# Hybrid S5 / differential attention / HGRN2 layer on one core: rows of x split and turned by DMA transposes, the norm's weight multiplied into the projection's weights, mixed channels loaded once per chunk

## The chip, the core and the metric

One core of a Trainium2 chip runs the whole program in one launch. The metric is the device time of an execution in microseconds, here the median of several runs. TensorE (PE) does the matmuls, VectorE (DVE), ScalarE (ACT) and GpSimd (POOL) the rest; SyncE (SP) issues most DMAs. Each engine works its instructions off in the order in which the program lists them for it.

## What is computed

One layer on x of 2048 rows and 1024 channels, in float32. The reference, cut to what matters:

```python
def rmsnorm(x, g):
    r = lax.rsqrt(jnp.mean(x * x, axis=-1, keepdims=True) + EPS)
    return x * r * g
...
h = rmsnorm(x, norm_mix_g[l])
proj = h @ w_in[l]
u, dq, dk, dv, cq, cf, ci, cg = split_projection(proj)   # 256, 3 x 384, 4 x 384 columns
y_a = s5_mixer(u, ...)
y_b = diff_attention(dq, dk, dv, ...)
y_c = hgrn2_mixer(cq, cf, ci, cg, ...)
mix = jnp.concatenate([y_a, y_b, y_c], axis=-1)
x = x + mix @ w_out[l]
h = rmsnorm(x, norm_ffn_g[l])
x = x + conv_glu_ffn(h, w_up, w_gate, conv_w, conv_b, w_down)
return rmsnorm(x, final_norm_g)
```

The change concerns h, the three places that multiply h by columns of w_in, and the product with w_out.

## The kernel before

**Products.** A float32 factor is held as two fp16 parts, a high part and the rest. `split` (L52) makes them: ACT writes the high part (L55), then DVE the low part in one operation (L63, or L61 where the scale is 1), or, with `pool=True`, POOL in two: a scaling in place (L58) and a subtraction (L59). `three` (L91, matmuls at L96) adds high x high, low x high and high x low. Weights are scaled by 1024 (`WS`) before the split, and results by its inverse.

**Order.** The program is written as generators that take turns, and a scheduler that works with a simulated timeline then fixes the order on every engine. Buffers come from pools with a fixed number each; who wants a buffer waits for its last reader.

**Stage A** (`phase_a`, L160) takes x in 16 row tiles of 128x1024, in four chunks j of 512 rows. `norm(j)` (L204) squares four tiles (ACT L216, two of the first chunk DVE L211), takes 1/sqrt (POOL's power at L72 and three small DVE operations), and scales the rows in place (ACT L227, DVE L229, POOL L233). Then PE turns each 128x128 block (L251, 8 blocks of 4 tiles a chunk) into PSUM tiles `a_pt`, which are split with the norm's weight g as scale (L255) into `a_h`: channels on partitions, tokens along the row. The chunk goes to DRAM as `Hd` (L259). For each of its tiles 24 matmuls (`a_pm`) give the 256 columns of u, which go to `Ud` (L269). `load_w` (L177) loads blocks of 128 columns of w_in into `a_wst` (two buffers) and splits them, two for u (`a_wu`) and nine for q, k and v (`a_w`). Between the tiles stand steps of the S5 branch: its parameters on DVE, and rotations of C on POOL (L537).

**QKV.** `proj` (L288) reads `Hd` chunk by chunk into `a_h2` (L291) and multiplies by `a_w` (`a_p`, to `QKd` and `Vd`). Beside it run the S5 branch, with its tables on POOL (L567 to L584) and its scans (tiles `s_w`, `s_ya`), and the splits of the first FFN weights.

**Attention and HGRN** are woven together. HGRN works in three passes `pr` over two heads each; at the start of a pass (`proj(u)`, j == 0) it loads four blocks of w_in (L1121) into `g_wst`, of which there is one buffer, and splits them into `g_w`, of which there is one, ACT first and DVE behind it (L1125). `load_h` (L1101) reads 256 tokens of `Hd` for each half chunk. The products are `g_pq` and `g_pv`. Attention turns its weights by DMA: `t_sc`, high and low part side by side, through `dma_start_transpose` into `t_wt` (L898).

**Second output projection.** The first FFN half runs, and within it `second` (L1960) makes the product with w_out for chunks 2 and 3. `project` (L1467) goes over two halves n of the output columns, and for each over four groups q of 256 channels: the mixed channels `o_y` are read from `Yd` (L1478, two DMAs), a block of w_out into `o_wst` (L1480) and split into `o_w` (L1488), then 24 matmuls follow (L1493). The rest is the second half of the FFN.

## Time and profile before

| | us |
|---|---|
| median of 3 runs | 2719.52 |
| lowest, highest run | 2718.45, 2723.11 |
| the profiled execution's own time | 2723.9 |
| its span (first to last instruction in the trace) | 2722.1 |
| mean granted TensorE clock | 0.934 |
| busy: PE, DVE | 2408.0, 1873.5 |
| busy: POOL, ACT | 1350.7, 1316.9 |

A line of the profile names the source line, the engine, the operation, the tile written and the tiles read ("a_h<-a_pt,a_g"), and the count; a group has the minimum, median and maximum of one instruction in ns. "[7.02 <-ACT g_w L55]" behind an instruction is idle time of its engine before it in us, and what ended it. A line "PE o_pm L1493: 16.9, 6" among waits gives us and how often. SPq is SP's queue of DMA issues. The table of stretches gives, for each, busy time of PE, its weight loads, DVE, ACT and POOL, the granted clock, the share of the 16 DMA engines, and GB/s.

### The profile page before, as it was taken

The numbers are of one execution on the slowest core, as the hardware profiler recorded it, in microseconds if no ns is written. First come the engines' busy times: TensorE is split into PE (matmuls) and PEld (weight loads), VectorE is DVE, ScalarE is ACT, GpSimd is POOL, SyncE is SP. The second block draws the span as 40 slices with busy tenths as digits, with TensorE's granted clock in tenths as the row PEclk, the third lists the DMA queues.
The fourth block names the chain that finished last, engine by engine and source line by source line (L and its number), as shares of the span: only waits on it lengthen the run. The fifth ranks groups of instructions, "written<-read, shape, count | busy, mean of one in ns | idle before, by whom it ended". The sixth has DMA issues, their size and how long they took to land.

```text
span 2722.1 us, 42584 instructions
## 1 busy us (share of the span) xinstructions
PE 2408.0 (88%) x15438; PEld 1354.2 (50%) x15438; DVE 1873.5 (69%) x3401; ACT 1316.9 (48%) x2470; POOL 1350.7 (50%) x1149
## 2 busy tenths in 40 slices
PE   5998898888888889769988898598979999999998
PEld 4655556766766764334443444243434444444444
DVE  7467756688869885597788998865455655545565
ACT  6333344667757663564466766633235433333321
POOL 5688612455444542367677677515313344444280
PEclk8899898888989989879999999699989999999999
DMA  7676555467456666655466665688784655554733
GB/s 240 230 214 207 167 161 126 94 133 143 104 125 137 132 135 177 161 122 182 150 182 169 183 173 170 207 276 256 266 312 148 204 168 154 155 148 136 286 99 123
DMA packets 556740, 473.07 MB, mean 174 GB/s; under 512 B 277297, under 2 KB 433265, under 8 KB 555505
## 3 DMA queue, kind: packets, MB, share of 16 engines
q1 hardware_dynamic: 534352, 429.97, 56.0%
q10 hardware_dynamic: 22176, 40.38, 4.0%
q8 instruction: 121, 1.98, 0.3%
q14 instruction: 91, 0.74, 0.1%
HBM read 290.35 MB, written 125.83 MB: 153 GB/s over the span
## 4 chain that ended last, share of the span: by engine, by line
PE 22%; DVE 15%; issue 8%; POOL 7%; ACT 7%; DMA 6%; SPq 1%; ACTq 0%; DVEq 0%; POOLq 0%
PE f_pd L1786 10%; PE f_pm L96 7%; POOL f_k L1863 2%; DVE f_a L61 2%; DMA f_dst<-in_w_down_dram 2%; DVE t_sc L836 2%; DVE f_t L1617 2%; PE o_pm L1493 2%; PE o_pe L1411 2%; DVE t_sc L867 1%; DVE f_w L63 1%; POOL f_u L1863 1%; ACT f_t L1615 1%; ACT f_t L1910 1%; ACT t_sc L848 1%
## 5 line engine op out<-in xcount | busy, mean ns | idle before, releaser
L96 PE MATMUL f_pm<-f_q,f_w 128*128 128x512 f16 x3696 | 836.8, 386 | 30.0 <-DVE f_u L1863 9.2
L96 PEld LDWEIGHTS <-f_w 128*128 128x128 f16 x3696 | 363.3, 99 | 487.5 <-issue 70.1
L1786 PE MATMUL f_pd<-f_dw,f_da 128*128 128x512 f16 x1848 | 407.1, 382 | 2.7 <-DVE f_r L1764 1.5
L891 POOL TENSOR_TENSOR t_sc<-t_sc 128x1024 f16<-128x1024 f32 (+7 forms) x144 | 250.6, 1753 | 302.3 <-ACT t_sc L890 279.1
L1786 PEld LDWEIGHTS <-f_da 128*128 128x128 f16 x1848 | 181.1, 98 | 226.2 <-issue 14.5
L832 PE MATMUL t_ps<-t_k,t_q 96*128 96x512 f16 (+2 forms) x480 | 165.9, 372 | 94.6 <-DVE t_mx L836 80.2
L848 ACT ACTIVATE t_sc<-t_sc,t_nm 128x128 f32<-128x128 f32 (+7 forms) x192 | 230.5, 1201 | 6.6 <-DVE f_a L61 1.1
L836 DVE CUSTOM_DVE_ANT_0 t_sc<-t_ps,t_base,t_mx 128x512 f32<-128x512 f32 (+3 forms) x288 | 185.2, 643 | 18.9 <-PE t_ps L832 10.8
L61 DVE TENSOR_TENSOR f_a<-f_t,f_a 128x512 f16<-128x512 f32 x132 | 154.8, 1192 | 48.3 <-ACT f_a L55 47.8
L913 PEld LDWEIGHTS <-t_wt 128*128 128x128 f16 x2448 | 106.3, 101 | 121.3 <-DMA t_wt<-t_sc 50.4
L867 DVE SCALAR_TENSOR_TENSOR t_sc<-t_sc,t_a 128x1024 f32<-128x1024 f32 (+7 forms) x144 | 164.6, 1169 | 1.6
L96 PE MATMUL g_pq<-g_h,g_w 128*128 128x256 f16 x1152 | 159.2, 299 | 5.1 <-DVE g_sg L1160 2.7
L1863 POOL TENSOR_TENSOR f_t<-f_t,f_t 128x512 f32<-128x512 f32 x66 | 101.6, 1553 | 123.1 <-ACT f_a L55 108.8
L913 PE MATMUL t_po<-t_v,t_wt 128*128 128x64 f16 x2448 | 120.5, 198 | 47.2 <-DMA t_wt<-t_sc 42.4
L96 PE MATMUL g_pv<-g_w,g_h 128*128 128x256 f16 x1152 | 150.3, 288 | 9.2 <-ACT g_w L55 9.2
L1863 POOL TENSOR_TENSOR f_k<-f_k,f_k 128x512 f32<-128x512 f32 x88 | 124.5, 1414 | 51.5 <-ACT f_halo L1907 25.4
L1617 DVE SCALAR_TENSOR_TENSOR f_t<-f_u,f_cw,f_t 128x1024 f32<-128x1024 f32 x88 | 124.1, 1410 | 33.1 <-ACT f_t L1615 32.3
L836 DVE CUSTOM_DVE_ANT_0 t_sc<-t_ps,t_base 128x512 f32<-128x512 f32 (+2 forms) x192 | 120.4, 631 | 34.4 <-PE t_ps L832 13.7
L890 ACT CAST t_sc<-t_sc 128x1024 f16<-128x1024 f32 (+7 forms) x144 | 111.4, 792 | 64.4 <-DVE t_sc L867 63.4
L55 ACT ACTIVATE f_w<-f_sum 128x512 f16<-128x512 f32 x110 | 69.2, 629 | 146.4 <-DVE f_sum L139 62.2
L96 PEld LDWEIGHTS <-g_w 128*128 128x128 f16 x1152 | 121.3, 107 | 36.2 <-issue 6.4
L96 PEld LDWEIGHTS <-g_h 128*128 128x128 f16 x1152 | 116.8, 103 | 36.8 <-issue 10.8
(335 smaller groups left out, 4475.4 us busy)
## 6 DMA issues: line engine op xcount, KB each, us to landing
f_w<-Wd SPq DMA_DIRECT2D x231, 256.0 KB, 3.0
Wd<-f_w SPq DMA_DIRECT2D x154, 256.0 KB, 2.1
Ad<-f_a ACTq DMA_DIRECT2D x154, 256.0 KB, 2.7
f_da<-Ad SPq DMA_DIRECT2D x42, 768.0 KB, 4.9
g_h<-Hd SPq DMA_DIRECT2D x24, 1024.0 KB, 6.7
f_dst<-in_w_down_dram SPq DMA_DIRECT2D x48, 512.0 KB, 4.9
...
```

The source lines that it names most:

```text
L61: nc.vector.tensor_tensor(out=lo, in0=src, in1=hi, op=ALU.subtract)
L96: nc.tensor.matmul(out=out, lhsT=lhs(a, k), rhs=rhs(b, k), start=(n == 0), stop=(n == 3 * nk - 1))
L832: nc.tensor.matmul(out=ps[:, 0:k1 - k0], lhsT=qt[:, c, 128 * (i % 4):128 * (i % 4) + 128], rhs=H.k[:, c, k0:k1], start=True, stop=True,)
L836: V.tensor_tensor_reduce(out=sc[c][:, k0:k1], in0=ps[:, 0:k1 - k0], in1=bs[:, k0:k1], scale=1.0, scalar=-3e38 if j == 0 else mx[:, c, j - ...
L848: nc.scalar.activation(out=sc[c][:, 0:L], in_=sc[c][:, 0:L], func=AF.Exp, scale=SLOPES[h], bias=nm[:, c:c + 1], accum_out=H.la[:, c, n_:n_ ...
L867: V.scalar_tensor_tensor(out=sc[0][:, k0:k1], in0=sc[1][:, k0:k1], scalar=a[:, 1:2], in1=sc[0][:, k0:k1], op0=ALU.mult, op1=ALU.add,)
L890: nc.scalar.copy(hl[:, k0:k1], sc[0][:, k0:k1])
L891: nc.gpsimd.tensor_tensor(out=hl[:, LM + k0:LM + k1], in0=sc[0][:, k0:k1], in1=hl[:, k0:k1], op=ALU.subtract,)
L913: nc.tensor.matmul(out=po, lhsT=wt[:, w, b, :], rhs=vt[:, b, 64 * v:64 * v + 64], start=(b == 0 and w + v == 0), stop=(b == i and w == 1),)
L1617: V.scalar_tensor_tensor(out=t0, in0=u[:, c:n + c], scalar=cw[:, c, m:m + 1], in1=t0, op0=ALU.mult, op1=ALU.add,)
L1786: nc.tensor.matmul(out=ps[t], lhsT=a[:, q, x, tk], rhs=w[:, y, q, :], start=(first and q + x + y == 0), stop=(last and q == n - 1 and y == 1),
L1863: eng.tensor_tensor(out=o, in0=a, in1=b, op=op)
```

## The change

**Stage A.** `turn(i)` takes the place of the transposes on PE: for each row tile ACT writes the high part of x·r and DVE the low part into `a_hl` (128x2048 fp16, three buffers), and one DMA transpose on SP turns the tile into `a_h`, with no norm weight in it. Norms are taken one tile at a time for the first four, then in pairs, all squares on ACT. x has seven buffers in place of eight; PSUM has four `a_pm` and no `a_pt`. In place of g in h, every block of w_in is multiplied by `gw` = 1024·g before its split (`scaled`), on POOL, or on DVE for the first block. `Hd` is stored as four tiles of [part, 128-channel group, 128 tokens] for each chunk; the matmuls that read 256 or 512 tokens read them in pieces of 128, and HGRN's reads get one contiguous piece per partition.

**HGRN.** Its 12 blocks get the same multiplication on POOL, in place in `g_wst`, ahead of the split.

**Second output projection.** `o_y` is loaded for n == 0 only, in four buffers instead of two, and `o_w` has two instead of three.

```diff
+    def scaled(self, f, eng):
+        eng.tensor_tensor(
+            out=f, in0=f, in1=self.gw.rearrange("p (k o) -> p k o", o=1).to_broadcast([128, KD, 128]),
+            op=ALU.mult,
+        )
...
# load_w in phase_a
-            K.split(dst[:, 0], dst[:, 1], f[:, :, 0:n], WS, pool=c0 > 0)
+            K.scaled(f, nc.gpsimd if c0 > 0 else nc.vector)
+            K.split(dst[:, 0], dst[:, 1], f[:, :, 0:n], 1.0, pool=c0 > 0)
...
-            xp = pool("a_x", 8)
+            xp = pool("a_x", 7)
+            lp = pool("a_hl", 3)
-            pt = pool("a_pt", 3, space=PSUM)
-            pm = pool("a_pm", 2, space=PSUM)
+            pm = pool("a_pm", 4, space=PSUM)
...
+            def turn(i):
+                j, t = divmod(i, 4)
+                if t == 0:
+                    hs[j] = hp.tile([128, 4, 2, KD, 128], F16, tag="h", name="a_h")
+                xt, r = xs.pop(i), rs.pop(i)
+                hl = lp.tile([128, 2, D], F16, tag="hl", name="a_hl")
+                nc.scalar.activation(out=hl[:, 0], in_=xt, func=AF.Copy, scale=r)
+                nc.vector.scalar_tensor_tensor(
+                    out=hl[:, 1], in0=xt, scalar=r, in1=hl[:, 0], op0=ALU.mult, op1=ALU.subtract
+                )
+                nc.sync.dma_start_transpose(
+                    out=hs[j][:, t].rearrange("p a k c -> p (a k) c"),
+                    in_=hl.rearrange("p a d -> p (a d)"),
+                )
+                load_x(i + 7)
...
-                        nc.tensor.transpose(
-                            ps[:, t * 128:t * 128 + 128], xs[4 * j + t][:, k * 128:k * 128 + 128],
-                            K.ident,
-                        )
-                    K.split(h[:, 0, k, :], h[:, 1, k, :], ps, g[:, k:k + 1])
...
+            for i in range(S // 128):
+                j, t = divmod(i, 4)
+                if i < 3:
+                    norm(i + 1, 1)
+                elif i % 2 and i + 1 < S // 128:
+                    norm(i + 1, 2)
+                if i + 1 < S // 128:
+                    turn(i + 1)
+                h = hs[j]
+                ps = pm.tile([128, 256], F32, tag="pm", name="a_pm")
+                three(nc, ps, lambda a, k: h[:, t, a, k, :], lambda b, k: wu[:, b, k, :], KD)
+                ut = op.tile([128, 256], F32, tag="u", name="a_u")
+                nc.scalar.activation(out=ut, in_=ps, func=AF.Copy, scale=IWS)
+                nc.sync.dma_start(out=Ud[128 * i:128 * i + 128, :], in_=ut)
+                if t == 3:
+                    nc.sync.dma_start(out=Hd[j], in_=hs.pop(j))
...
# load_h and proj(u) in HGRN
-            nc.sync.dma_start(out=h, in_=Hd[j, :, :, :, 256 * a:256 * a + 256])
+            nc.sync.dma_start(out=h, in_=Hd[j, :, 2 * a:2 * a + 2])
-                    K.split(w[:, 0, :, cc], w[:, 1, :, cc], f, WS)
+                    K.scaled(f, nc.gpsimd)
+                    K.split(w[:, 0, :, cc], w[:, 1, :, cc], f)
...
# project and second
+                if n == 0:
+                    y = yp.tile([128, 2, 2, CH], F16, tag="y", name="o_y")
+                    for k in range(2):
+                        nc.sync.dma_start(
+                            out=y[:, k], in_=Yd[2 * q + k, :, :, j * CH:(j + 1) * CH])
+                    ys[q] = y
+                y = ys[q]
-            yp, wp, st = pool("o_y2", 2, "left"), pool("f_w2", 3, "left"), pool("f_st2", 2, "left")
+            yp, wp, st = pool("o_y2", 4, "left"), pool("f_w2", 2, "left"), pool("f_st2", 2, "left")
```

The scheduler puts the instructions in another order. Three places follow, before and after. First, SP's queue at the end of stage A (`a_h_1430`, `a_h_2235`, and after the change `a_h_1310`, `a_h_2115`, are the first two chunks read back for QKV). Before:

```order
32 L259 DMA Hd<-a_h 128x8192
33 L269 DMA Ud<-a_u 128x256 x4
34 L179 DMA a_wst<-in_w_in_dram 128x8x128 x2
35 L291 DMA a_h_1430<-Hd 128x8192
36 L291 DMA a_h_2235<-Hd 128x8192
37 L259 DMA Hd<-a_h 128x8192
```

and after:

```order
62 L188 DMA a_wst<-in_w_in_dram 128x8x128
63 L242 DMA_TRANSPOSE a_h<-a_hl 128x16x128 x2
64 L188 DMA a_wst<-in_w_in_dram 128x8x128
65 L272 DMA Ud<-a_u 128x256
66 L274 DMA Hd<-a_h 128x8192
67 L272 DMA Ud<-a_u 128x256
68 L188 DMA a_wst<-in_w_in_dram 128x8x128
69 L296 DMA a_h_1310<-Hd 128x8192
70 L272 DMA Ud<-a_u 128x256
71 L296 DMA a_h_2115<-Hd 128x8192
```

The first read of `Hd` has moved from ahead of the last chunk's write to behind it, and behind the last two transposes and the last block of w_in.

Second, POOL at the start of HGRN, where the first pass's weights come (`g_mk`, `t_base`: masks and positions). Before:

```order
360 L1036 MEMSET g_ones 128x512
361 L1046 AFFINE_SELECT g_mk<-g_ones 128x64 x2
362 L1050 AFFINE_SELECT g_mk<-g_mk 128x64 x2
363 L1046 AFFINE_SELECT g_mk<-g_ones 128x64
364 L1058 AFFINE_SELECT g_mk_3689<-g_ones 128x128
365 L1050 AFFINE_SELECT g_mk<-g_mk 128x64
366 L1062 AFFINE_SELECT g_mk_3689<-g_mk_3689 128x128
367 L715 IOTA t_base 128x2048
```

and after:

```order
362 L70 TENSOR_TENSOR g_wst<-g_wst,gw 128x1024
363 L1041 MEMSET g_ones 128x512
364 L1051 AFFINE_SELECT g_mk<-g_ones 128x64 x2
365 L1055 AFFINE_SELECT g_mk<-g_mk 128x64 x2
366 L1051 AFFINE_SELECT g_mk<-g_ones 128x64
367 L1063 AFFINE_SELECT g_mk_3569<-g_ones 128x128
368 L1055 AFFINE_SELECT g_mk<-g_mk 128x64
369 L1067 AFFINE_SELECT g_mk_3569<-g_mk_3569 128x128
370 L70 TENSOR_TENSOR g_wst<-g_wst,gw 128x1024 x4
371 L720 IOTA t_base 128x2048
```

Five multiplications by `gw` now stand there, four of them in a row ahead of `t_base`; the fifth belongs to the second pass.

Third, SP's queue in the second output projection. Before:

```order
689 L1480 DMA o_wst<-in_w_out_dram 128x2x512
690 L1995 DMA f_r<-Xd 128x1024
691 L1478 DMA o_y<-Yd 128x2x512 x2
692 L1995 DMA f_r<-Xd 128x1024
693 L1480 DMA o_wst<-in_w_out_dram 128x2x512
694 L1478 DMA o_y<-Yd 128x2x512 x2
695 L1480 DMA o_wst<-in_w_out_dram 128x2x512
696 L1478 DMA o_y<-Yd 128x2x512 x2
697 L1480 DMA o_wst<-in_w_out_dram 128x2x512
698 L1478 DMA o_y<-Yd 128x2x512 x6
```

and after:

```order
707 L1488 DMA o_y<-Yd 128x2x512 x2
708 L1971 DMA Xd<-o_r 128x1024
709 L1493 DMA o_wst<-in_w_out_dram 128x2x512
710 L2008 DMA f_r<-Xd 128x1024
711 L1493 DMA o_wst<-in_w_out_dram 128x2x512
712 L2008 DMA f_r<-Xd 128x1024 x3
713 L1493 DMA o_wst<-in_w_out_dram 128x2x512 x3
714 L1971 DMA Xd<-o_r 128x1024 x4
```

Where two reads of `o_y` stood between one block of w_out and the next, the blocks now follow each other, and the last `o_y` is read four blocks earlier.

More of the change, by code (lines that the diff above doesn't have):

```diff
@@ L46, in __init__ @@
         make_identity(nc, self.ident)
+        self.gw = const.tile([128, KD], F32, name="gw")
         self.mhalf = const.tile([128, 1], F32, name="mhalf")
@@ L167, in phase_a @@
         st = es.enter_context(tc.tile_pool(name="a_st", bufs=2))
-        g = wp.tile([128, KD], F32, name="a_g")
-        nc.sync.dma_start(out=g, in_=norm_g[0].rearrange("(k p) -> p k", p=128))
+        nc.sync.dma_start(out=K.gw, in_=norm_g[0].rearrange("(k p) -> p k", p=128))
+        nc.vector.tensor_scalar(out=K.gw, in0=K.gw, scalar1=WS, scalar2=None, op0=ALU.mult)
         qs = wp.tile([128, 3], F32, name="a_qs")
@@ L202, in load_x, with norm @@
                     xs[i] = xt
-            def norm(j):
+            def norm(i, n):
                 ss = sp.tile([128, 4], F32, tag="ss", name="a_ss")
-                for t in range(4):
-                    sq = sp.tile([128, D], F32, tag="sq", name="a_sq")
-                    xt = xs[4 * j + t]
-                    if j == 0 and t % 2:
-                        nc.vector.tensor_tensor_reduce(
-                            out=sq, in0=xt, in1=xt, scale=1.0, scalar=0.0, op0=ALU.mult, op1=ALU.add,
-                            accum_out=ss[:, t:t + 1],
-                        )
-                    else:
-                        nc.scalar.activation(
-                            out=sq, in_=xt, func=AF.Square, accum_out=ss[:, t:t + 1]
-                        )
+                for t in range(n):
+                    sq = sp.tile([128, D], F16, tag="sq", name="a_sq")
+                    nc.scalar.activation(
+                        out=sq, in_=xs[i + t], func=AF.Square, accum_out=ss[:, t:t + 1]
+                    )
@@ L238, in phase_a @@
-            for i in range(4):
+                    out=v[:, 0:n], in0=ss[:, 0:n], scalar1=1.0 / D, scalar2=EPS, op0=ALU.mult,
+                    op1=ALU.add,
+                )
+                r = K.rsqrt(sp, v[:, 0:n], n, f"r{n}")
+                for t in range(n):
+                    rs[i + t] = r[:, t:t + 1]
+            def turn(i):
[11 more added lines that the diff above has]
+                    in_=hl.rearrange("p a d -> p (a d)"),
+                )
+                load_x(i + 7)
@@ new lines, in phase_a @@
+            for i in range(S // 128):
[14 more added lines that the diff above has]
+                    nc.sync.dma_start(out=Hd[j], in_=hs.pop(j))
+                for _ in range(2):
+                    with tc.high_priority(offset=-300):
+                        params = params and next(s5)
+                for n in range(9 * i // 16, 9 * (i + 1) // 16):
+                    load_w(w[:, :, :, 128 * n:128 * n + 128], 256 + 128 * n, 128)
@@ L289, in proj @@
             for j in range(NCH):
-                h = hp.tile([128, 2, KD, CH], F16, tag="h", name="a_h2")
+                h = hp.tile([128, 4, 2, KD, 128], F16, tag="h", name="a_h2")
                 nc.sync.dma_start(out=h, in_=Hd[j])
@@ L1104, in load_h @@
             j, a = (n % 8) // 2, n % 2
-            h = hp.tile([128, 2, KD, 256], F16, tag="h", name="g_h")
-            nc.sync.dma_start(out=h, in_=Hd[j, :, :, :, 256 * a:256 * a + 256])
+            h = hp.tile([128, 2, 2, KD, 128], F16, tag="h", name="g_h")
+            nc.sync.dma_start(out=h, in_=Hd[j, :, 2 * a:2 * a + 2])
             hts[n] = h
@@ L1475, in project @@
             for q in qs:
-                y = yp.tile([128, 2, 2, CH], F16, tag="y", name="o_y")
-                for k in range(2):
-                    nc.sync.dma_start(out=y[:, k], in_=Yd[2 * q + k, :, :, j * CH:(j + 1) * CH])
+                if n == 0:
[5 more added lines that the diff above has]
+                y = ys[q]
                 f = st.tile([128, 2, 512], F32, tag="wst", name="o_wst")
@@ L2027 @@
     K = Ctx(tc, const)
-    Hd = tc.dram_tile([NCH, 128, 2, KD, CH], F16, name="Hd")
+    Hd = tc.dram_tile([NCH, 128, 4, 2, KD, 128], F16, name="Hd")
     QKd = tc.dram_tile([2, 2, NH * HD, S], F16, name="QKd")
```

64 lines of the change are left out of this document (15 added, 49 removed).

## The prediction

> **What bounds the kernel now.** I read the page first, then busy time by stage, then single tiles and stretches of the timeline in the stages that the change touches. The page's first lines:
>
> ```profile
> span 2722.1 us, 42584 instructions
> PE 2408.0 (88%) x15438; PEld 1354.2 (50%) x15438; DVE 1873.5 (69%) x3401; ACT 1316.9 (48%) x2470; POOL 1350.7 (50%) x1149
> ```
>
> TensorE is 88% busy, so whatever is saved must be idle TensorE time, 314 us in all. The stages have different limits, so the next view is the table of busy time by stretch: its bounds, its length, then busy time of PE, weight loads, DVE, ACT and POOL, the granted clock, DMA share and GB/s.
>
> ```profile
> 0.00:20.00 20.00, 3.56 (x14) 2.64 (x14) 6.97 (x17) 11.58 (x17) 9.62 (x19) 1.00 0.88 271
> 20.00:40.00 20.00, 13.44 (x56) 8.19 (x56) 14.97 (x45) 11.44 (x18) 12.69 (x7) 0.75 0.64 177
> 40.00:60.00 20.00, 14.68 (x115) 12.06 (x116) 19.97 (x100) 12.92 (x21) 7.65 (x6) 0.93 0.62 197
> 60.00:80.00 20.00, 18.25 (x154) 15.32 (x154) 19.93 (x44) 14.19 (x24) 10.36 (x7) 0.98 0.78 291
> 80.00:100.00 20.00, 17.37 (x122) 15.39 (x120) 15.10 (x25) 7.92 (x15) 16.82 (x12) 0.79 0.49 172
> 149.00:349.00 200.00, 172.62 (x924) 106.75 (x922) 142.53 (x213) 71.15 (x135) 155.60 (x293) 0.93 0.63 196
> 2110.00:2515.00 405.00, 401.69 (x1848) 181.23 (x1848) 217.75 (x263) 142.85 (x238) 179.28 (x142) 0.99 0.54 162
> ```
>
> The first stage, which the change rewrites, waits for x and the norm until about 20 us; from 40 to 80 DVE is busy for 39.9 of 40 us, so DVE bounds it. From 2110 on PE has 401.7 of 405 us: nothing that the change does can be gained there. The first 100 us hold 100 − 67.3 = 32.7 us of idle PE.
>
> **First stage: transposes by DMA.** The removed work, by tile:
>
> ```profile
> L251 PE MATMUL a_pt<-ident,a_x x128: 272/273/476, 14.7 to 98.8; 128*128 128x128 f32 x128
> L96 PE MATMUL a_pm<-a_wu,a_h x384: 272/273/421, 20.0 to 112.5; 128*128 128x256 f16 x192
> L63 DVE SCALAR_TENSOR_TENSOR a_h<-a_pt,a_g,a_h x32: 733/739/751, 20.7 to 100.0; 128x512 f16<-128x512 f32 x32
> L211 DVE CUSTOM_DVE_ANT_0 a_sq<-a_x x2: 1225/1226/1226, 6.6 to 9.4; 128x1024 f32<-128x1024 f32 x2
> L229 DVE TENSOR_SCALAR a_x<-a_x,rs_y x2: 753/1140/1528, 13.8 to 14.5; 128x1024 f32<-128x1024 f32 x2
> 12.11 1.23 DVE L63 SCALAR_TENSOR_TENSOR a_wu<-a_wst,a_wu 128x1024 f16<-128x1024 f32 x1 [1.23 <-ACT a_wu L55]
> 13.45 0.16 DVE L84 TENSOR_TENSOR rs_t<-rs_t,a_v 128x4 f32<-128x4 f32 x1
> ```
>
> PE loses 128 × 0.273 = 35 us, but PE is not what bounds this stage. DVE loses 32 × 0.739 = 23.6, 2 × 1.23 = 2.5 and 2 × 1.14 = 2.3 us. It gains 16 low halves of 128x1024; the same instruction on a weight block took 1.23 us, so 16 × 1.23 = 19.7; ten norms instead of four, each of four small operations of 0.16: 6 × 0.64 = 3.8; and one scaling of the first weight block, some 1.2. Net −28.4 + 24.7 = −3.7 us. So the DVE bound hardly moves; the DMA side is new. One transposed tile is 128x2048 fp16, 512 KB. The nearest rows are the attention's own transposes of the same shape; one of them stood alone in this stretch:
>
> ```profile
> 1500.30:1504.80 4.50, 4.50 (x22) 1.95 (x20) 4.50 (x7) 3.94 (x6) 2.49 (x3) 0.91 0.61 117
> 1500.37 1.76 SPq L898 DMA_TRANSPOSE t_wt<-t_sc  x1
> L898 SPq DMA_TRANSPOSE t_wt<-t_sc x2: 1756/2206/2656, 1493.6 to 1500.4; - x2
> DMA to landing us min/median/max: 4.3/5.0/5.7
> ```
>
> It kept the 16 DMA engines busy for 0.61 × 4.5 = 2.75 us, held SP's queue for 1.76 us, and the two landed after 4.3 and 5.7 us. Sixteen of them add 16 × 2.75 = 44 us of all DMA engines. If 1.76 us, the issue time, were the real rate, it would be 28 us; I take 44, because it is the busy time itself. The first 100 us already use 0.88, 0.64, 0.62, 0.78 and 0.49 of 20 us each, 68 us. 68 + 44 = 112 us would not fit into 100, but about 10 us of the 68 lie behind the last transpose, so DMA needs some 102 us. The dependent loop gives about the same: transposes and everything else stand in one SP queue, 16 × (4.5 to land + about 1 for a store in front) = 88, behind a first tile at about 12, is 100 us. Hence the last tile is turned between 90 and 105 us where the last low half now is written at 100.8 us.
>
> What follows is the QKV projection, which needs the stored h of chunk 0 and the last weight block. Its first and last matmuls, and what stands ahead of them:
>
> ```profile
> 99.29 1.66 SPq L291 DMA_DIRECT2D a_h<-Hd  x2
> 101.04 1.37 SPq L259 DMA_DIRECT2D Hd<-a_h  x1
> 101.02 2.77 POOL L58 TENSOR_SCALAR a_wst<-a_wst 128x1024 f32<-128x1024 f32 x1 [1.50 <-ACT a_w L55]
> 103.87 2.12 POOL L59 TENSOR_TENSOR a_w<-a_wst,a_w 128x1024 f16<-128x1024 f32 x1
> 112.60 3.62 PE L96 MATMUL a_p<-a_h,a_w 128*128 128x512 f16 x16
> 409.75 2.44 PE L96 MATMUL a_p<-a_w,a_h 128*128 128x384 f16 x14
> ```
>
> Before, the two reads of Hd stood ahead of the last write of Hd on SP; now the first read stands behind the last write, which waits for the last transpose, and behind a weight load. So PE starts the projection at about 90 to 105, plus 17 us (4.5 for the tile to land, 24 U matmuls of 0.27 or 6.6, some 6 for the read behind the write to land): 107 to 122 instead of 112.6. On POOL the scaling by gw replaces a scaling by a constant that took 2.77 us; the nearest row for two tensors at this shape is the 2.12 us above; I take 2.4, no loss.
>
> Whether PE's start sets the end of the projection is a question of the S5 chain beside it. POOL is busy for 155.6 of the 200 us from 149 on, and DVE and POOL wait for each other there:
>
> ```profile
> POOL s_w L625 <- DVE s_w L421: 20.9, 12, 6.8
> PE s_pu L594 <- DVE s_w L421: 18.8, 4, 8.2
> 92.11 2.47 POOL L537 TENSOR_TENSOR s_t<-s_c,s_col 128x256 f32<-128x256 f32 x4 [2.36 <-DVE s_qp L421]
> ```
>
> PE's 172.6 of 200 leaves 27 us of slack there, 18.8 of it behind S5. The chain's first POOL rotation starts at 92.1; in the new order it stands behind DVE copies that come between the low halves of tiles 13 and 14, so at 82 to 95. I take 4 us earlier for that chain and 4 us later for PE, with the chain deciding more often: −3 us at the end of the stage, between −12 (both early by the 10 us of the lower bound) and +12 (the read of Hd behind a full DMA queue).
>
> **The price of a transpose, again.** Plain transfers of this stage set the other bound:
>
> ```profile
> 60.00:66.00 6.00, 5.96 (x51) 5.28 (x51) 5.93 (x10) 5.32 (x12) 5.92 (x3) 0.94 1.07 430
> ```
>
> At 430 GB/s 512 KB take 1.2 us, so 16 tiles would cost 19 us in place of 44, and DMA would need 77 us in place of 102: 25 us less for the first stage. The 2.75 us of the attention's transpose stand against it, and the sum goes by them. The Trainium skill, page "Advanced Engine Details and Errata", section "X-Bar Transpose (TRN2)", sides with the smaller price: it says that transposing DMAs on this chip are as fast as regular ones. By that rule the sum would be rival 1's.
>
> The projection's matmuls now read h in four runs of 128 columns, which no row shows; I take nothing for it, since PE's 27 us of slack would hold 0.03 us more on each of some 900 matmuls.
>
> **HGRN weights.** Its 12 blocks get a POOL operation between landing and split, in a buffer of which there is one, so a cycle grows by that operation. The rows of the cycle:
>
> ```profile
> 411.91 1.06 ACT L55 ACTIVATE g_w<-g_wst 128x1024 f16<-128x1024 f32 x1 [3.87 <-DMA g_wst<-in_w_in_dram]
> 418.11 1.06 ACT L55 ACTIVATE g_w<-g_wst 128x1024 f16<-128x1024 f32 x1 [4.27 <-DMA g_wst<-in_w_in_dram]
> 419.21 7.00 PE L96 MATMUL g_pv<-g_w,g_h 128*128 128x256 f16 x48 [7.02 <-ACT g_w L55]
> PE g_pv L96: 9.2, 3
> ```
>
> A block takes 418.11 − 411.91 = 6.2 us now, and about 8.6 with 2.4 more: 4 × 2.4 = 9.6 us a reload, 29 us for three. In this trace PE was held by it for 9.2 us, 7.0 of them in the first reload, where the PE had run out of projection. In the new order more of the QKV projection is left for PE to do around that reload; the second and third lie under attention, and there PE lost 9.2 − 7.0 = 2.2 us in two waits. Queued behind the POOL operation, which waits for the block to land, are the masks and t_base at the first reload and the attention's subtractions (which its transposes wait for) at the later ones. At the first reload five of them stand ahead of t_base, the fifth for a block that can only be loaded when the fourth is split: about 2.3 for that split, 4 to land and 2.4 to multiply, 8.7 us behind the fourth ACT split, where PE's 7.0 us of g_pv hide most of it. I take a third of 29, +9 us, between 0 and +28.
>
> **Second output projection.** o_y is loaded once instead of twice, 16 of 32 loads go. What PE waited for (the last two rows are those of o_wst: its landing, and ACT's waits for PE to release a split buffer):
>
> ```profile
> DMA o_y<-Yd: 16.9, 6
> L1478 SPq DMA_DIRECT2D o_y<-Yd x32: 517/600/1247, 1904.8 to 2063.1; - x32
> 2010.44 5.35 PE L1493 MATMUL o_pm<-o_w,o_y 128*128 128x512 f16 x24 [1.21 <-DMA o_y<-Yd]
> DMA to landing us min/median/max: 3.7/7.2/9.9
> PE o_pm L1493: 15.6, 2
> ```
>
> PE waited 16.9 us in six places. With half the loads gone and four buffers, only the first load of each tile is left; chunk 3's are issued while chunk 2's second half runs. What is late next: o_wst, whose splits then have two buffers instead of three; ACT already waited 15.6 us for one. I take −13, between 0 and −17.
>
> **Smaller.** The HGRN reads of Hd become contiguous, 8 KB a partition in place of 512 B pieces; PE waited 1.2 us for one, and SP and the DMA engines are eased: −2, between 0 and −4.
>
> ```profile
> PE g_pq L96 <- DMA g_h<-Hd: 1.2, 1, 1.2
> ```
>
> **Sum.** −3 + 9 − 13 − 2 = −9 us on the profiled execution's 2723.9 (span 2722.1): 2715. The median of the runs is 2719.5, 4.4 below it, so 2710.5, say 2710.
>
> **Rivals.** (1) A larger gain: transposes run at the plain rate, 1.2 us a tile, 19 us in place of 44; then the first stage ends some 25 us earlier and DVE (−3.7) is freed of waiting for x: −25 + 9 − 13 − 2 = −31, 2688. The 430 GB/s stretch speaks for it, the 2.75 us row against: 0.12. (2) Slower: the HGRN reload is uncovered. PE does wait 7.0 us there in this trace, so each added 2.4 us may pass on to it (3 × 9.6 = 29): −3 + 29 − 13 − 2 = +11, 2730. It decides from the point where more than 18 us of the 29 reach PE; the 2.2 us of both later reloads speak against: 0.2. (3) No change: o_wst takes o_y's place (the two buffers; a landing of up to 9.9 us against 5.35 us of matmuls a step), so 0 in place of −13: −3 + 9 − 2 = +4, 2723: 0.18. My forecast has 0.5.
>
> **How the numbers follow.** A measurement of this kernel can tell about 0.2%, 5.4 us, from no change. Of the forecast's 0.5, 0.36 lies more than that below 2719.5, 0.12 within and 0.02 above; rival 1 adds 0.12 to faster; of rival 2, 0.17 is slower and 0.03 within; of rival 3, 0.11 is within and 0.07 slower. That is 0.48 faster, 0.26 the same and 0.26 slower. The range reaches from 2690, the forecast with its stage term at −12 and the HGRN term at 0 (−27, 2692) and a little of rival 1, to 2732, just above rival 2. The forecast's own range is 2697 to 2724.
>
> **What would show it.** First stage: QKV's first matmul between 107 and 122 us, a transpose's DMA busy time of 2.2 to 2.75 us. HGRN: a gap of 8 to 9 us between the ACT splits of g_w, and PE's wait for g_w above 9.2 us in all. Second projection: no wait of over 2 us for o_y from 1980 on. I am wrong if the projection's last matmul falls before 400 us (now 412), if PE's waits for g_w exceed 25 us, or if PE's wait in the second projection stays above 10 us under another name.

## The result, and the profile after

The changed kernel takes 2752.97 us (median of 4 runs, 2745.51 to 2762.26) where the kernel before takes 2720.12 (4 runs, 2718.45 to 2723.11): it is slower, the ratio is 1.0128 (95% interval 1.0106 to 1.015). The forecast was 2710, with a range of 2690 to 2732.

The profiled execution took 2750.49 us. The page's first lines, of the changed kernel:

```profile
span 2748.8 us, 42282 instructions
PE 2405.1 (87%) x15310; PEld 1347.8 (49%) x15310; DVE 1891.5 (69%) x3405; ACT 1306.9 (48%) x2450; POOL 1367.0 (50%) x1161
```

128 matmuls are gone. They were 25.2 us of PE's busy time; the 35 us of the prediction added up durations that overlap. Yet PE is busy for 2405.1 us, only 2.9 less than before, so the other matmuls took 22.3 us longer. The mean granted clock of this execution was 0.926, that of the one before 0.934; an estimate from these figures, (2408.0 − 25.2) × 0.934 / 0.926 = 2403 us, comes close to the 2405.1. PE's idle time grew from 314.1 to 343.7 us. The first stage by stretches, with the same columns as before (the last three are the granted clock, the DMA share and GB/s):

```profile
0.00:20.00 20.00, 0.51 (x2) 0.36 (x2) 12.23 (x22) 13.60 (x19) 9.79 (x22) 1.00 0.88 255
20.00:40.00 20.00, 13.38 (x87) 10.04 (x88) 17.82 (x97) 10.31 (x16) 6.27 (x6) 0.95 1.09 246
40.00:60.00 20.00, 10.50 (x59) 7.29 (x57) 10.47 (x47) 7.46 (x11) 5.50 (x4) 0.71 1.10 280
60.00:80.00 20.00, 10.05 (x72) 7.59 (x72) 6.95 (x11) 9.03 (x14) 5.56 (x5) 0.89 1.04 290
80.00:100.00 20.00, 8.11 (x52) 5.94 (x52) 9.31 (x16) 4.84 (x6) 8.00 (x4) 0.76 0.91 152
100.00:120.00 20.00, 14.25 (x79) 10.35 (x79) 18.94 (x41) 4.28 (x6) 5.33 (x5) 0.68 1.00 269
120.00:140.00 20.00, 9.65 (x80) 8.12 (x80) 0.42 (x1) 3.82 (x5) 20.00 (x23) 0.75 0.96 346
```

The reader sees the bound change hands. DVE, 39.9 of 40 us busy before, now has 17.4 of the 40 from 40 to 80; the DMA share, 0.49 to 0.88 before, stands at 0.88 to 1.10 all the way to 140. The waits of PE, the transposes as a group (ns on SP), and three places of the timeline (a long transpose, the first POOL rotation of the S5 branch, QKV's first matmuls):

```profile
PE a_pm L104 <- DMA a_h<-a_hl: 40.5, 12, 9.5
```

```profile
L242 SPq DMA_TRANSPOSE a_h<-a_hl x16: 1889/3610/10788, 17.9 to 117.5; - x16
```

```profile
72.49 10.79 SPq L242 DMA_TRANSPOSE a_h<-a_hl  x1
...
118.69 2.47 POOL L542 TENSOR_TENSOR s_t<-s_c,s_col 128x256 f32<-128x256 f32 x4 [8.26 <-DVE s_qp L426]
...
138.53 21.71 PE L104 MATMUL a_p<-a_h,a_w 128*128 128x512 f16 x88 [10.35 <-DMA a_h<-Hd]
```

PE waited 40.5 us for transposes, and QKV's first matmul is at 138.5 instead of 112.6: 26 us, about as much as the span has grown (26.7). Between, the trace shows two more losses and a gain: QKV's last matmul is at 448.2 (411.9 before), HGRN's last g_pv at 1022.1 (983.6), attention's last t_ps at 1921.5 (1879.5), the second projection's last o_pm at 2103.2 (2072.5). The lag is 26, 36, 39, 42 and 31 us at these places. How far such a start scatters can be seen in e4_oy_once, e5_hgrn_scale, e7_tiny and e11_halves below: the source of their first stage is that of the kernel before, and QKV's first matmul is at 107.0, 109.9, 107.1 and 113.4 there, with a granted clock of 0.90, 0.91, 0.94 and 0.88 up to that point (112.6 and 0.88 in the kernel before). A shift of 6 us in this start means little.

HGRN's first reload and the second projection in the changed kernel's timeline, and POOL's waits from 400 to 900:

```profile
425.70 8.45 PE L104 MATMUL a_p<-a_w,a_h 128*128 128x384 f16 x51
431.62 1.06 ACT L56 ACTIVATE g_w<-g_wst 128x1024 f16<-128x1024 f32 x1 [5.12 <-POOL g_wst L70]
440.21 1.06 ACT L56 ACTIVATE g_w<-g_wst 128x1024 f16<-128x1024 f32 x1 [6.78 <-POOL g_wst L70]
441.31 6.74 PE L104 MATMUL g_pv<-g_w,g_h 128*128 128x256 f16 x48 [3.29 <-ACT g_w L56]
...
2030.66 31.50 PE L1506 MATMUL o_pm<-o_w,o_y 128*128 128x512 f16 x136 [1.13 <-DVE o_w L64]
2063.62 19.15 PE L1506 MATMUL o_pm<-o_w,o_y 128*128 128x512 f16 x88 [1.46 <-ACT o_w L56]
```

```profile
POOL g_wst L70 <- DMA g_wst<-in_w_in_dram: 54.7, 8, 10.1
```

The last cycle of a block at the first reload is 8.6 us, as forecast; the others of the three reloads, from the starts of the same ACT splits, are 8.6 to 15.5 us. From the first split to the last, the reloads took 25.0, 21.4 and 23.0 us before and take 29.7, 31.1 and 36.5 now, 27.9 more in all, close to the forecast's 29. POOL stands 54.7 us in eight waits for blocks to land, with all that is queued behind it. PE waits 3.3 us for g_pv at the first reload instead of 7.0, because the program still has QKV matmuls (a_p) for it there. In the second projection runs of 136 and 88 matmuls stand where PE stopped for o_y in six places.

### The profile page after: what moved, and what is told of

Same layout as the page of the kernel before. It is cut to its first block, busy times and chain, and to the rows that moved or that the text cites. A ratio compares the mean times of both kernels' runs of the same rounds, so it can differ in the third digit from the quotient of the medians.

```text
span 2748.8 us, 42282 instructions
## 1 busy us (share of the span) xinstructions
PE 2405.1 (87%) x15310; PEld 1347.8 (49%) x15310; DVE 1891.5 (69%) x3405; ACT 1306.9 (48%) x2450; POOL 1367.0 (50%) x1161
## 5 line engine op out<-in xcount | busy, mean ns | idle before, releaser
L104 PE MATMUL f_pm<-f_q,f_w 128*128 128x512 f16 x3696 | 838.4, 387 | 25.1 <-DVE f_u L1876 9.8
L918 PE MATMUL t_po<-t_v,t_wt 128*128 128x64 f16 x2448 | 121.3, 202 | 35.9 <-DMA t_wt<-t_sc 32.9
L104 PE MATMUL g_pq<-g_h,g_w 128*128 128x256 f16 x1152 | 148.7, 287 | 2.9 <-DVE g_sg L1167 1.6
L104 PE MATMUL a_p<-a_h,a_w 128*128 128x512 f16 x576 | 137.1, 393 | 13.3 <-DMA a_h<-Hd 10.3
L841 DVE CUSTOM_DVE_ANT_0 t_sc<-t_ps,t_base 128x512 f32<-128x512 f32 (+2 forms) x192 | 120.2, 631 | 40.2 <-PE t_ps L837 22.3
L1630 DVE SCALAR_TENSOR_TENSOR f_t<-f_u,f_cw,f_t 128x1024 f32<-128x1024 f32 x88 | 122.4, 1391 | 33.7 <-ACT f_t L1628 32.9
```

Source lines behind the costliest of these rows:

```text
L104: nc.tensor.matmul(out=out, lhsT=lhs(a, k), rhs=rhs(b, k), start=(n == 0), stop=(n == 3 * nk - 1))
L841: V.tensor_tensor_reduce(out=sc[c][:, k0:k1], in0=ps[:, 0:k1 - k0], in1=bs[:, k0:k1], scale=1.0, scalar=-3e38 if j == 0 else mx[:, c, j - ...
L918: nc.tensor.matmul(out=po, lhsT=wt[:, w, b, :], rhs=vt[:, b, 64 * v:64 * v + 64], start=(b == 0 and w + v == 0), stop=(b == i and w == 1),)
L1630: V.scalar_tensor_tensor(out=t0, in0=u[:, c:n + c], scalar=cw[:, c, m:m + 1], in1=t0, op0=ALU.mult, op1=ALU.add,)
```

## The experiments

Times are medians. Each difference is to the kernel before in the same series, since that moves by some us from one series to the next (2716.9 to 2721.1). An interval of the last column is 6 to 21 us wide. A difference of two such differences is therefore known to some 7 to 12 us either way, an estimate from these widths: below, 1.9 and 6.9 us can't be told from nothing, and 13.0 hardly.

| kernel | us | difference to before | 95% interval of the ratio |
|---|---|---|---|
| changed kernel | 2753.0 | +32.9 | 1.0106 to 1.015 |
| e1_plain | 2742.0 | +25.1 | 1.0052 to 1.0106 |
| e3_two_queues | 2782.0 | +65.2 | 1.019 to 1.0269 |
| e10_twice | 2808.8 | +89.3 | 1.0297 to 1.0346 |
| e9_no_hgrn | 2752.0 | +31.0 | 1.008 to 1.0143 |
| e14_turn_only | 2743.8 | +24.1 | 1.0058 to 1.0109 |
| e15_turn_hgrn | 2755.6 | +37.1 | 1.0098 to 1.0173 |
| e4_oy_once | 2710.1 | −6.8 | 0.9959 to 0.9991 |
| e6_layout | 2703.5 | −17.6 | 0.9918 to 0.9957 |
| e5_hgrn_scale | 2756.6 | +39.7 | 1.0112 to 1.0163 |
| e12_e6_hgrn | 2742.9 | +23.4 | 1.0051 to 1.0109 |
| e7_tiny | 2729.5 | +8.4 | 1.0014 to 1.0036 |
| e11_halves | 2742.4 | +21.3 | 1.0064 to 1.01 |
| e13_gw_stage_a | 2722.0 | +2.5 | 0.9992 to 1.0022 |

### The first stage: price of the transposes, or queue

**Plain copies.**

```diff
# changed kernel, turn()
-                nc.sync.dma_start_transpose(
-                    out=hs[j][:, t].rearrange("p a k c -> p (a k) c"),
+                nc.sync.dma_start(
+                    out=hs[j][:, t].rearrange("p a k c -> p (a k c)"),
                     in_=hl.rearrange("p a d -> p (a d)"),
```

> The changed kernel with each of the 16 transposes of the first stage replaced by a plain copy of the same 512 KB in 4 KB runs; the turning is left out, so its output is not the layer's. Theory A (the DMA engines are the bound of the first stage, and a transpose is dear because it goes in 256-byte packets, 47 us of all engines for the 16): a copy at the plain rate costs 1.2 to 1.8 us of all engines, 19 to 29 us in all, so the stage shortens by 18 to 28 us: QKV's first matmul at 110 to 120 us instead of 138.5, total 2725 to 2735. Theory B (SP's queue is the bound, held 1.9 to 10.8 us by each transpose): a copy holds SP about 0.6 us, some 60 us of SP time go, and QKV starts at about 110 too; the DMA share in the first 120 us would then fall well below 0.9. Theory C (the loss comes from elsewhere, HGRN's weights above all): QKV's start falls but the total stays within 5 us of 2753.

The plain copies' kernel: stretches from 40 to 80 us, and QKV's first group of matmuls with its first and last start:

```profile
40.00:60.00 20.00, 12.73 (x96) 9.95 (x95) 19.90 (x63) 12.34 (x20) 8.95 (x6) 0.86 1.03 386
60.00:80.00 20.00, 6.82 (x55) 5.37 (x52) 19.41 (x43) 6.93 (x11) 8.79 (x4) 0.76 0.62 240
```

```profile
L104 PE MATMUL a_p<-a_h,a_w x576: 379/379/634, 125.6 to 417.5; 128*128 128x512 f16 x192
```

QKV starts at 125.6, 12.9 us earlier, less than expected: the engines move 386 GB/s where they moved 280, the share falls to 0.62 behind, and DVE is the bound again (39.3 of 40 us). So about half of the 26 us goes with the turning: up to 140 us 42784 packets of under 512 bytes move in the changed kernel, 14118 with the copies and 9777 before. The other half stands with 8 MB more that pass through a stage in which DMA was busy for most of the time, with the multiplications (e14_turn_only below, without them, starts QKV 3.9 us earlier) and with the new order; this run does not part them. Nor does it part theories A and B, since a copy also held SP for only 0.5 us in the median. The total fell by only 7.8 us against the changed kernel, less than either of them expected. The Trainium skill's section "X-Bar Transpose (TRN2)" (page "Advanced Engine Details and Errata"), weighed in the prediction, would have the plain copies make next to no difference; the 12.9 us speak against it in this stage.

**Another queue.**

```diff
# changed kernel: the loads of x, the stores of u and of h in the first stage
-nc.sync.dma_start(...)
+nc.scalar.dma_start(...)
```

> The changed kernel with the loads of x and the stores of u and h of the first stage issued from ScalarE's DMA queue; the transposes and the loads of weights stay on SP. Same bytes, same packets. Theory A (DMA engines full): QKV's first matmul stays at 135 to 142 us and the total within 6 us of 2753, the DMA share of the first 120 us at about 1.0. Theory B (order and holding of SP's queue): the transposes no longer stand behind 2 MB stores, QKV starts 15 to 25 us earlier, total 2728 to 2738.

The kernel with two queues: SP's timeline, one stretch, and QKV's matmuls:

```profile
27.88 50.35 SPq L242 DMA_TRANSPOSE a_h<-a_hl  x7
```

```profile
60.00:80.00 20.00, 6.59 (x31) 4.41 (x32) 9.61 (x30) 4.38 (x7) 0.81 (x1) 0.59 1.18 159
```

```profile
L104 PE MATMUL a_p<-a_h,a_w x576: 379/379/634, 153.9 to 439.5; 128*128 128x512 f16 x192
```

Neither theory had this number: QKV starts 15.4 us later. Ten of them are there before anything is turned: the first transpose is issued at 27.9 instead of 17.9 us. ACT's queue issues seven loads of x first, for 9.1 us, and ACT's first square of x starts at 18.0 instead of 5.4:

```profile
0.78 9.09 ACTq L211 DMA_DIRECT2D a_x<-in_x_dram  x7
18.00 1.04 ACT L219 ACTIVATE a_sq<-a_x 128x1024 f16<-128x1024 f32 x1
```

From the first transpose to QKV's first matmul it is 126.0 us here and 120.6 in the changed kernel. With the plain traffic of the stage gone from SP, seven transposes in a row hold it for 50 us, 7.2 us each, while the DMA share is 1.18 at only 159 GB/s. So the plain transfers that stood in SP's queue were not what held QKV up, against theory B. What SP loses to the transposes themselves was not tested apart.

**Twice.**

```diff
# changed kernel, turn()
+                for _ in range(2):
+                    nc.sync.dma_start_transpose(...)
-                nc.sync.dma_start_transpose(...)
```

> The changed kernel with each of the 16 transposes of the first stage issued twice, the same tile into the same place. Theory A (the DMA engines are the bound; 16 transposes are some 47 us of all of them): QKV's first matmul 40 to 55 us later than 138.5, at 178 to 194, total 2785 to 2808. Rival (latency of single transposes, with engines to spare): 16 landings of 4.4 to 6 us more in the loop, some of them hidden, QKV at 150 to 170.

The kernel with each transpose twice: the stretch from 20 to 100 us, and QKV's matmuls:

```profile
20.00:100.00 80.00, 34.09 (x192) 24.51 (x192) 32.73 (x150) 25.41 (x39) 16.16 (x12) 0.76 1.09 258
```

```profile
L104 PE MATMUL a_p<-a_h,a_w x576: 379/379/634, 179.5 to 461.8; 128*128 128x512 f16 x192
```

16 more transposes put QKV's start off by 41.0 us, 2.6 us each, and the total by 56.4, to just above theory A's range. The latency of single transposes, the rival, is out. The price is close to the 2.75 us that the prediction took from the attention's transpose. The run does not part the engines' time from that of SP's queue: all transposes together held SP for 73.5 us in the changed kernel and for 109.1 here.

**The transposes alone, and the multiplications of the first stage alone.** Both stand beside e6_layout below, which has the o_y edit and the layout and nothing else.

```diff
# e14_turn_only: changed kernel, load_w and HGRN
-            K.scaled(f, nc.gpsimd if c0 > 0 else nc.vector)
-            K.split(dst[:, 0], dst[:, 1], f[:, :, 0:n], 1.0, pool=c0 > 0)
+            K.split(dst[:, 0], dst[:, 1], f[:, :, 0:n], WS, pool=c0 > 0)
...
-                    K.scaled(f, nc.gpsimd)
-                    K.split(w[:, 0, :, cc], w[:, 1, :, cc], f)
+                    K.split(w[:, 0, :, cc], w[:, 1, :, cc], f, WS)
# e13_gw_stage_a: e6_layout with gw = 1024 everywhere, load_w
-            K.split(dst[:, 0], dst[:, 1], f[:, :, 0:n], WS, pool=c0 > 0)
+            K.scaled(f, nc.gpsimd if c0 > 0 else nc.vector)
+            K.split(dst[:, 0], dst[:, 1], f[:, :, 0:n], 1.0, pool=c0 > 0)
```

> The changed kernel without any multiplication by gw: weights are split with scale 1024 as before, in the first stage and in HGRN, so the norm's weight is left out; the transposes by DMA, the layout and the o_y edit stay. Beside the kernel with the o_y edit and the layout (2703.5) it shows the transposes alone. Theory A (the DMA engines are the bound of the first stage): QKV's first matmul at 130 to 140 us, total 2738 to 2755, little less than with the first stage's multiplications. Rival (the multiplications in the first stage and the transposes share the loss about evenly, as 18 us of the former alone suggest): QKV's first matmul at 118 to 128, total 2722 to 2737.

> The kernel with o_y loaded once and the new layout of h, and in addition the first stage's weight blocks multiplied by a broadcast tile (1024 everywhere) on POOL, in place of POOL's multiplication by a constant; x is still turned on PE. Theory A (the DMA traffic of the transposes is what costs in the first stage): within 6 us of 2703.5, QKV's first matmul at 104 to 112 us. Rival (the multiplications of the first stage's weights on POOL are part of its loss): QKV's first matmul later than 118 us, 2715 or more.

QKV's first matmul in e14_turn_only, then in e13_gw_stage_a, and ACT's wait in the latter:

```profile
L104 PE MATMUL a_p<-a_h,a_w x576: 379/379/634, 134.6 to 412.1; 128*128 128x512 f16 x192
```

```profile
L105 PE MATMUL a_p<-a_h,a_w x576: 376/379/634, 117.7 to 391.9; 128*128 128x512 f16 x192
```

```profile
ACT a_w L57 <- POOL a_wst L71: 8.4, 5, 3.4
```

The transposes alone cost 24.1 + 17.6 = 41.7 us beside e6_layout, as theory A had it. At QKV's first matmul the lag behind e6_layout is 27.0 us (134.6 against 107.6), at its last 39.0, at HGRN's last g_pv 22.1 and at attention's last t_ps 41.3; what makes the part behind QKV's start, no run shows.

The multiplications of the first stage cost 2.5 + 17.6 = 20.1 by themselves, against the expectation of theory A that they cost nothing: QKV starts 10.1 us later than e6_layout's 107.6, of which some 6 may be scatter. The cause stays open. POOL's constant scaling stood behind ACT's split before, the multiplication stands ahead of it, and ACT waits 8.4 us for it; but in e6_layout ACT waited 12.6 us for the same blocks to land, so this wait is no loss. What grew is PE's wait at `a_pt` for DVE's low parts of h, from 7.1 to 16.6 us: DVE, the bound of the stage, also multiplies the first block now, for 1.23 us, and works in another order. On top of the transposes (e9_no_hgrn against e14_turn_only) the same multiplications cost 31.0 − 24.1 = 6.9 us.

### HGRN's multiplications

```diff
# e5_hgrn_scale: kernel before, with gw = 1024 everywhere; e12_e6_hgrn: the same on e6_layout
-                    K.split(w[:, 0, :, cc], w[:, 1, :, cc], f, WS)
+                    K.scaled(f, nc.gpsimd)
+                    K.split(w[:, 0, :, cc], w[:, 1, :, cc], f)
# e7_tiny: kernel before
+                    nc.gpsimd.tensor_scalar(
+                        out=f[:, :, 0:1], in0=f[:, :, 0:1], scalar1=1.0, scalar2=None, op0=ALU.mult)
# e11_halves: e5_hgrn_scale, load, multiply and split for z in range(2)
+                        kk = slice(4 * z, 4 * z + 4)
...
+                        K.split(w[:, 0, kk, cc], w[:, 1, kk, cc], f[:, kk])
# e9_no_hgrn: changed kernel; e15_turn_hgrn: e14_turn_only with the first three lines of this diff
-                    K.scaled(f, nc.gpsimd)
-                    K.split(w[:, 0, :, cc], w[:, 1, :, cc], f)
+                    K.split(w[:, 0, :, cc], w[:, 1, :, cc], f, WS)
```

> The kernel before with one addition: HGRN's 12 weight blocks are multiplied on POOL by a broadcast tile, ahead of the split, which then has scale 1; the tile holds 1024 everywhere, so what is computed is unchanged. The prediction's term: +9 us (2729), bounds 0 and +28. From the changed kernel's trace, where a block's cycle is 8.6 to 10 us instead of 6.2 and PE waits 5.3 us for g_pv instead of 9.2: +3 to +10, 2723 to 2730. Theory C (this is where the changed kernel loses): +25 or more, 2745.

> The kernel with o_y loaded once and the new layout of h (first stage as before, on PE), and in addition HGRN's 12 multiplications on POOL (by 1024). Theory E (a delay in HGRN is paid in full where PE has no other work, and is hidden where the first stage is late and leaves QKV work to do beside the reload): about as much as on the kernel before, +25 to +40 over 2703.5, so 2728 to 2744. Rival (the +40 measured on the kernel before was the other order of that one program): within 12 us of 2703.5.

They cost 39.7 us on the kernel before and 23.4 + 17.6 = 41.0 on e6_layout: more than the 29 of the prediction's second rival. The rival that the order of one program was to blame is answered only in part, because the two programs stand in the same order at the first reload. ACT's, DVE's and SP's rows for the third block there, and ACT's for the fourth, in e12_e6_hgrn:

```profile
413.56 1.06 ACT L57 ACTIVATE g_w<-g_wst 128x1024 f16<-128x1024 f32 x1 [3.64 <-POOL g_wst L71]
417.72 1.22 DVE L63 TENSOR_TENSOR g_w<-g_wst,g_w 128x1024 f16<-128x1024 f32 x1
418.97 0.40 SPq L1130 DMA_DIRECT2D g_wst<-in_w_in_dram  x1
425.67 1.04 ACT L57 ACTIVATE g_w<-g_wst 128x1024 f16<-128x1024 f32 x1
```

DVE writes the low part 4.2 us behind ACT, with attention's preparations (`t_lv`, `t_gc`, `t_base`) ahead of it, and only then is the fourth block loaded. The fourth split stands 12.1 us behind the third (12.4 in e5_hgrn_scale); in the changed kernel, whose order is another, it is 8.6. PE at the same place:

```profile
407.37 1.92 PE L105 MATMUL g_pq<-g_h,g_w 128*128 128x256 f16 x16 [0.21 <-DVE g_w L63]
417.36 0.61 PE L841 MATMUL t_ps<-t_k,t_q 96*128 96x128 f16 x3 [8.07 <-DMA t_q<-QKd]
419.34 2.22 PE L841 MATMUL t_ps<-t_k,t_q 96*128 96x256 f16 x5 [1.38 <-DVE t_mx L845]
423.95 0.61 PE L841 MATMUL t_ps<-t_k,t_q 96*128 96x512 f16 x1 [2.39 <-DMA t_q<-QKd]
426.75 7.59 PE L105 MATMUL g_pv<-g_w,g_h 128*128 128x256 f16 x48 [2.20 <-ACT g_w L57]
```

PE has used up QKV (its last matmul starts at 404.7) and has 0.61 + 2.22 + 0.61 = 3.4 us of work between 409.3 and 426.8. Yet its waits for g_w fell, to 2.2 us at g_pv (9.3 in e6_layout); this time stands under other names, attention's loads and maxima. And most of the price is no wait at all. Of the 43.4 us between the spans of the two traces (2697.2 and 2740.6), 13.6 are idle PE (298.9 and 312.5) and 29.8 are busy PE (2398.3 and 2428.1, page below and here) for the same 15438 matmuls:

```profile
span 2740.6 us, 42534 instructions
PE 2428.1 (89%) x15438; PEld 1362.4 (50%) x15438; DVE 1891.1 (69%) x3402; ACT 1316.8 (48%) x2470; POOL 1378.7 (50%) x1161
```

The mean granted clock was 0.937 there and 0.926 here; 2398.3 × 0.937 / 0.926 = 2427 us is an estimate from these figures. Over the three reloads it was 0.95, 0.79 and 0.84 in e6_layout and 0.81, 0.74 and 0.69 in e12_e6_hgrn. The third reload, first in e6_layout, then in e12_e6_hgrn:

```profile
775.40:797.00 21.60, 19.17 (x162) 13.93 (x163) 17.25 (x47) 10.68 (x19) 2.95 (x4) 0.84 0.39 119
802.60:838.30 35.70, 29.05 (x239) 19.54 (x238) 34.25 (x85) 22.07 (x43) 20.23 (x15) 0.69 0.39 88
```

Whether the clock fell because of the delays, no run tests; it fell where they are. Whoever prices a delay by the waits for that tile alone reads too little. On POOL the multiplication, 1.9 us, waits for the landing with everything behind it (the group, then POOL's waits from 400 to 900 us, in e12_e6_hgrn):

```profile
L71 POOL TENSOR_TENSOR g_wst<-g_wst,gw x12: 1895/1896/2245, 391.2 to 834.1; 128x1024 f32<-128x1024 f32 x12
```

```profile
POOL g_wst L71 <- DMA g_wst<-in_w_in_dram: 37.5, 9, 7.4
```

> The kernel before with a very small POOL operation (eight elements a partition, times 1) on each of HGRN's 12 weight blocks between landing and split. Theory D1 (what costs is the length that the multiplication adds to the chain of load, multiply, split in one buffer): about 0.2 to 0.4 us a block, total 2716 to 2724. Rival D2 (what costs is standing in POOL's queue behind the attention's and HGRN's own operations, or the other order of the program): most of the +40 remains, 2740 or more.

> The kernel before with HGRN's multiplications on POOL (by 1024, so nothing computed changes), but each block is loaded, multiplied and split in two halves within the same buffer: the same POOL work in 24 operations of half the size, while the two halves overlap. Theory D1 (length of the chain): the cycle of a block falls from about 9 us towards 6.5, total 2717 to 2730. Rival D2 (POOL's work and queue): 2745 or more, as much as with whole blocks (2757).

The tiny operation, which waits in POOL's queue just the same, costs 8.4 us, so the other 31 come with the 1.9 us of work in each block's chain, or with the order that e5_hgrn_scale got. Halves cost 21.3, although the last two cycles of the first reload fell to 7.9 and 6.6 us, as theory D1 had it (6.6 and 6.4 in e6_layout, without multiplications). Both totals lie between the two theories: the length of the chain is not all of it, and the shares of chain, queue and order were not parted. How much of the halves' 21.3 is POOL's work and how much the 24 smaller loads was not separated.

> The changed kernel without HGRN's 12 multiplications by gw on POOL; its weights are split with scale 1024 as before, so HGRN's products lack the norm's weight. Theory D (two losses: the first stage some 17 to 26 us, HGRN's reload some 20 to 30; the second projection gives 7 to 12 back): 20 to 30 us less than the changed kernel's 2753, 2723 to 2733, with HGRN's ACT splits about 6.2 us apart again. Rival (the first stage alone, HGRN as small as the prediction's +9): 2744 or more.

> The changed kernel without the multiplication of the first stage's weights; HGRN's multiplications and the transposes by DMA stay (the first stage's products lack the norm's weight). Beside it stands the kernel with the transposes alone, 24.1 us above the kernel before on its own chip run. Theory E (HGRN's multiplication is hidden where the transposes have made the first stage late): within 8 us of that, 16 to 32 us above the kernel before. Rival F (its price is there as well, 30 to 41 us, and it was the removal from the changed kernel that met something else): 50 us or more above the kernel before.

In the changed kernel, leaving them out gains 1.9 us, within the scatter of either (2745 to 2762), as the rival of e9_no_hgrn had it. With the transposes alone they cost 37.1 − 24.1 = 13.0, between the ranges of theory E and rival F. So the price is smaller in the programs with transposes. The rows of the changed kernel at 425.70 and 441.31 show QKV matmuls under the reload that e12_e6_hgrn no longer has, and its cycles there are not stretched by attention's preparations. Both belong to the order that the scheduler gave these programs; that the first stage is late on the chip does not by itself change it. That fits the first reload. For the second and third it is not settled; e9_no_hgrn is 11 us ahead of the changed kernel at HGRN's end (1011.0 against 1022.1) and has lost that at attention's end (1920.4 against 1921.5), and no run shows why.

### The second projection, and the layout

```diff
# e4_oy_once: kernel before, with project() and second() of the changed kernel
# e6_layout: e4_oy_once, and
-    Hd = tc.dram_tile([NCH, 128, 2, KD, CH], F16, name="Hd")
+    Hd = tc.dram_tile([NCH, 128, 4, 2, KD, 128], F16, name="Hd")
-                    K.split(h[:, 0, k, :], h[:, 1, k, :], ps, g[:, k:k + 1])
+                    K.split(h[:, :, 0, k, :], h[:, :, 1, k, :], ps.rearrange("p (t c) -> p t c", t=4),
+                            g[:, k:k + 1])
...
```

> The kernel before with the second output projection's edit alone (o_y loaded once a chunk, its buffers 2 to 4, the w_out split's 3 to 2). The prediction's term: 13 us less than before, 2707, with no wait of PE for o_y from 1980 us on. The changed kernel's trace has 11.5 us less in this stretch: 2708 to 2710. Rival (w_out blocks take over the wait): within 4 us of 2720.

> The kernel before with o_y loaded once a chunk and with the stored h laid out as in the changed kernel (HGRN reads one contiguous piece a partition, matmuls read h in runs of 128 columns); the first stage still turns x on PE and nothing is multiplied on POOL. The prediction's terms: 2 us less than with the o_y edit alone, 2705 to 2709. Rival (the matmuls that read h in runs of 128 columns are slower: 576 took 393 ns in the changed kernel, 383 before): 4 us or more above the o_y edit alone, 2714 or more.

The second projection in e4_oy_once, and the page of e6_layout:

```profile
1979.09 3.57 PE L1498 MATMUL o_pm<-o_w,o_y 128*128 128x512 f16 x8 [5.47 <-ACT o_w L55]
2016.66 19.15 PE L1498 MATMUL o_pm<-o_w,o_y 128*128 128x512 f16 x88 [1.71 <-ACT o_w L55]
```

```profile
span 2697.2 us, 42545 instructions
PE 2398.3 (89%) x15438; PEld 1350.4 (50%) x15438; DVE 1884.1 (70%) x3401; ACT 1317.0 (49%) x2470; POOL 1353.4 (50%) x1149
```

The o_y edit gains 6.8 us: the waits for o_y are gone, and 5.47 + 1.71 = 7.2 us of waits for w_out's split have come in their place, as the third rival had it in part. All of PE's waits at o_pm fell from 17.4 to 10.0 us. The layout brings more than forecast, 17.6 in all, and no run shows by what; matmuls that read runs of 128 columns are not slower (379 ns in the median in both). e6_layout is the fastest kernel of this study, 0.9937 of the kernel before (0.9918 to 0.9957): the change without its transposes and without its multiplications.

## Why the prediction was wrong

**The stage term, −3 us, is the step that failed.** Three of its parts did.

1. The sum of DMA time. "68 + 44 = 112 us would not fit into 100, but about 10 us of the 68 lie behind the last transpose" counted only what passes before the last tile is turned. QKV waits for more: the last store of h, its reading back and the last weight blocks. Up to QKV's start the kernel before, and then the changed kernel, have

```profile
0.00:112.00 112.00, 79.31 (x545) 63.96 (x546) 78.11 (x228) 60.13 (x94) 68.06 (x58) 0.88 0.71 236
0.00:138.50 138.50, 64.98 (x422) 49.10 (x422) 76.14 (x232) 52.29 (x75) 58.95 (x62) 0.82 1.00 261
```

0.71 × 112 = 79.5 us of all engines before. With the prediction's own 44 us that makes 123.5 us ahead of QKV even if no engine ever stood idle, and the forecast of 107 to 122 lay below it. The share of 1.00 over 138.5 us shows engines that were busy throughout, with 59 us added instead of 44. The price of one transpose, 2.75 us, agrees with the 2.6 of the doubling; where the other 15 us come from (dearer transposes, or dearer plain traffic beside them), no run parts.

2. "4 us earlier for that chain", "with the chain deciding more often". The chain's first rotation came at 118.7, not at 82 to 95, because the loads of C stand on SP behind the eleventh transpose (SP reached them at 89.0), and SP was held 1.9 to 10.8 us by each transpose where the prediction counted 1.76. So the chain and PE's start were both late by 26 us (92.1 and 112.6 before). Which of them would have decided alone is not shown; PE stood idle for 31.7 us between QKV's first and last matmul before, and for 32.3 after.

3. "No loss" for the multiplication of the first stage's weights. The operation is shorter than the old one, 1.9 us instead of 2.77, and still costs 20 us alone. Beside the transposes its 6.9 us can't be told from nothing. By which way it costs, no run shows.

The prediction's signs of being wrong did not warn: QKV's last matmul was not before 400 us (448.2), PE's waits for g_w were not above 25 us (5.3 at g_pv), and the wait in the second projection was not above 10 (8.5). The number that told was QKV's first matmul.

**HGRN, +9 in the range of 0 to +28.** The reloads grew by 27.9 us, close to the 29 of the forecast, and in the changed kernel their price is 1.9, which the scatter does not tell from 9. The reason given, QKV matmuls beside the reload, is there at the first reload. For the other two it is not shown, so that the small price is in part luck. Where the program's order left PE no QKV matmuls the price was 40 us, above the upper bound: the share was taken from PE's waits for g_w, and e12_e6_hgrn has 13.6 us more of idle PE and 29.8 us more of busy PE for the same matmuls, and for the latter the prediction had no term.

**The second projection, −13, measured −6.8:** o_w's waits took half. **Layout, −2:** measured 17.6 − 6.8 = 11 (two series). Both signs were right; the 2 us rested on one wait of 1.2 us, which can't be the source of 11.

**The rivals.** The first is out: 16 more transposes cost 2.6 us each, not 1.2. The second was passed by what HGRN's multiplications do by themselves, but it is not what the changed kernel lost by. The third came in part. Put one after another, the differences read 41.7 + 6.9 + 1.9 − 17.6 = 32.9: transposes, first multiplications, HGRN's, and what the rest gains. This sum closes by construction, and it depends on the order: with HGRN's multiplications put in first (e15_turn_hgrn) they are 13.0 and the first stage's −4.2. Among the losses only the transposes' 41.7 stands well clear of the scatter.
